# Nested self-attention with ragged lengths: V projected by key tile instead of by head pair

## The chip, the cores and the metric

The kernel runs on one core of a Trainium2 chip. The metric is the device time in microseconds (us) of one execution. Four compute engines work side by side on that core: PE multiplies matrices and writes PSUM, ACT does the exponentials and some copies, DVE does most of the copies out of PSUM and the normalisation, POOL casts inputs. SP and ACT issue the DMAs. PEld is the row of the profile for PE's weight loads, which run beside its matmuls.

## The reference

32 sequences of up to 512 rows and 512 columns; each has a length drawn between 64 and 511, and only its first rows count. Eight heads of 64 columns each.

```python
for b in range(batch):
    seq_len = lengths[b]
    qkv = np.matmul(x[b, :seq_len], w_qkv)
    q, k, v = np.split(qkv, 3, axis=-1)          # then split into 8 heads of 64
    scores = scale * np.matmul(q, k.transpose(0, 2, 1))
    attn = np.exp(scores - np.max(scores, axis=-1, keepdims=True))
    attn = attn / (np.sum(attn, axis=-1, keepdims=True) + 1e-08)
    output[b, :seq_len] = np.matmul(attn, v).transpose(1, 0, 2).reshape(seq_len, dim)
```

Rows past a sequence's length stay zero.

## The kernel before

**Sequences and classes.** The kernel sorts the sequences by length on the chip and takes them in pairs, longest first. Each pair belongs to a class N, the longer length rounded up to a multiple of 32; T is the number of 128-row key tiles in N. For this draw the 16 pairs are: two with T = 4 (N = 512 and 448), six with T = 3 (384, three times 352, 320, 288), six with T = 2 (256, twice 224, 192, twice 160) and two with T = 1 (128, 96). Each class has its own code, a body, which loops while pairs of its class come.

**Halves.** A body does two halves, h = 0 and h = 1, one for each sequence of the pair. In half h the kernel does the attention of sequence h and, between its steps, the projections of the next sequence (g = 1 - h) into the other set of buffers. So what is projected in one half is used in the next.

**Steps.** Within a half the order of PE's work is written out by hand as a string of tokens, `ORDER` for T = 4, 3 and 2 and `DENSE` for T = 3 where three score blocks fit into two PSUM banks (N = 320 and 288):

- `S`: scores of one unit of the current pair of heads into one of two PSUM slots (`psc`, slots s0 and s1), and their exponential by ACT into `ep`. The units come in the order of pairs 1, 2, 3 of this sequence and then pair 0 of the next. `D` does all three key tiles of a pair at once and needs both slots.
- `Q`, `K`: projection of Q or K of one head pair by `qk` (weights are the stationary operand, x the streamed one) into one of two banks of `pa` (a0, a1), and a copy into `qkT`. `B` does Q and K of a pair together. An upper-case letter has the copy done by DVE, a lower-case one by ACT.
- `V`: projection of V by `vproj`, and DVE's copy into `v_aug` with a mask.
- `A`: attention times V of one head pair by `attnv` into `pav`, and DVE's normalisation: a reciprocal and products into `onat`. With T = 3 and 2 the pairs 0 and 1, and 2 and 3, share one normalisation, which follows the odd one. `+` interleaves the matmuls of `A` with those of the step before. With `R` and `X` tokens the normalisation is put at a later place.
- `O`, `P`: ACT waits for the normalisation and issues the store of one half of the columns. With T = 3 and 4 SP issues the second store.

**What orders the engines.** Each projection token takes the other bank of `pa` than the one before it (`st["bank"] ^= 1`), in `group`: PE waits until the bank's last copy is done (`acquire`), does the matmuls, and DVE or ACT waits for them. So each projection waits for the copy of the projection two tokens earlier. Each engine takes its own work strictly in the order of the tokens: ACT's exponentials, copies and the waits of `O` and `P` stand in one queue, as do DVE's copies and normalisations. `pav` has no semaphore of its own; that it is free again follows from the copies that DVE does behind the normalisation.

**V before the change.** `vproj(pr, bank, h, i, T)` does one pair of heads over all T key tiles: T x 4 matmuls that stream 128 columns each, 16 with T = 4, 12 with T = 3 and 8 with T = 2. Four such tokens make up a half. With T = 1 one token does all heads, in 4 matmuls of 512 streamed columns. The matmuls run at line 248 of the profile like all others (a helper); the copy is line 390, with T = 1 line 370; copies of Q and K are line 357 (DVE) and 355 (ACT), exponentials line 290 (in `D` 322), the normalisation lines 447, 469 and 471, the store on ACT line 908.

Of the kernel before, what the change touches and what calls it, by code (L numbers as in the profile page):

```python
# [11 lines left out]
ALU = mybir.AluOpType  # L12

P = 128
NH = 8
HD = 64
# [91 lines left out]
def kernel(  # L108
# [9 lines left out]
    B, MAXS, D = x.shape  # L118
    NT = MAXS // P
    NC = D // P  # L120
# [5 lines left out]
    def sb(name, shape, dt):  # L126
        return nc.alloc_sbuf_tensor(name, shape, dt).ap()
# [5 lines left out]
    w_r = sb("w_r", [P, NC, 3 * D], F16)  # L133
    x_nat = [sb(f"x_nat_{h}", [P, NT, D], FP32) for h in range(2)]
    x16 = [sb(f"x16_{h}", [P, NT, D], F16) for h in range(2)]
    xT = [sb(f"xT_{h}", [P, NC, MAXS], F16) for h in range(2)]
    qkT = [sb(f"qkT_{h}", [P, 2 * NPAIR, MAXS], F16) for h in range(2)]
    v_aug = [sb(f"v_aug_{h}", [P, NT, NH, HD + 1], F16) for h in range(2)]
# [31 lines left out]
    pa = nc.alloc_psum_tensor("pa", [P, 2, MAXS], FP32).ap()  # L170
# [51 lines left out]
    now = [None]  # L222

    def acquire(pr, b):
        if pr.busy.get(b):
            pr.take("pe", free[b])
            pr.busy[b] = False

    def close(pr, b, eng, mms):
        k = len(mms) - 1  # L230
        carry, pr.signals = pr.signals[:k], pr.signals[k:]
        raises = {j: [sem] for j, sem in enumerate(carry)}
        raises[k] = [full[(b, eng)]]
        pr.add("pe", Matmuls(mms, raises))

    def group(pr, b, eng, mms, evac):
        if b in free:
            acquire(pr, b)
        close(pr, b, eng, mms)
        pr.take(eng, full[(b, eng)])  # L240
        if b in free:
            pr.add(eng, lambda e: evac(e).then_inc(free[b], 1))
            pr.busy[b] = True
        else:
            pr.add(eng, evac)

    def mm(o, lhsT, rhs, start, stop):
        return lambda e: e.matmul(o, lhsT, rhs, start=start, stop=stop)  # L248
# [107 lines left out]
        else:  # L356
            group(pr, b, eng, mms, lambda e: e.tensor_copy(out=dst, in_=src))  # L357

    def vproj(pr, bank, h, i, T):
        b = f"a{bank}"  # L360
        mms = []
        if T == 1:
            for c in range(NC):
                mms.append(
                    mm(pa[:, bank, :], xT[h][:, c, 0:P], w_r[:, c, 2 * D : 3 * D],
                       c == 0, c == NC - 1)
                )
            group(
                pr, b, "dve", mms,
                lambda e: e.tensor_scalar(  # L370
                    out=v_aug[h][:, 0, :, 0:HD],
                    in0=pa[:, bank].rearrange("p (h d) -> p h d", d=HD),
                    scalar1=now[0][:, 0, 0:1], scalar2=None, op0=ALU.mult,
                ),
            )
            return
        for t in range(T):
            for c in range(NC):
                mms.append(
                    mm(  # L380
                        pa[:, bank, t * P : (t + 1) * P],
                        xT[h][:, c, t * P : (t + 1) * P],
                        w_r[:, c, 2 * D + i * P : 2 * D + (i + 1) * P],
                        c == 0,
                        c == NC - 1,
                    )
                )
        group(
            pr, b, "dve", mms,
            lambda e: e.tensor_tensor(  # L390
                out=v_aug[h][:, 0:T, 2 * i : 2 * i + 2, 0:HD],
                in0=pa[:, bank, 0 : T * P].rearrange("p (t a d) -> p t a d", a=2, d=HD),
                in1=now[0][:, 0, 0:T].unsqueeze(2).unsqueeze(3).broadcast_to([P, T, 2, HD]),
                op=ALU.mult,
            ),
        )
# [92 lines left out]
    def spread_last(pr):  # L489
# [8 lines left out]
    CANON = {b: True for b in banks}  # L498

    ORDER = {  # L500
# [3 lines left out]
    }  # L504
    DENSE = "D Q0 K0 A0 V0 D Q1 A1 k1 V1 D Q2 K2 A2 V2 D Q3 A3 k3 V3 O"

    ahead = {}

    def read_class(pr, h):
        if h == 0:  # L510
            for g in ("pe", "act", "dve"):
                pr.add(g, lambda e: next_class(e))
# [13 lines left out]
    def half(pr, h, T, N, st):  # L526

        g = 1 - h
        pr.signals += [s_vf[g]] if T == 1 else [s_xtf[h], s_vf[g]]

        def start_proj():
            if not st["x"]:
                st["x"] = True
                pr.take("pe", s_xt[g], 64)
                pr.signals.append(s_x16f[g])

        if T == 1:
            start_proj()
            qk(pr, st["bank"], g, [(i, 0) for i in range(NPAIR)], N, P)
            qk(pr, st["bank"] ^ 1, g, [(i, 1) for i in range(NPAIR)], N, P, "act")  # L540
            read_class(pr, h)
            pr.take("pe", s_on[h])
            attnv(pr, h, 0, 1)
            vproj(pr, st["bank"], g, 0, 1)
            fetch_far(pr, h, N)
            acquire(pr, f"a{st['bank'] ^ 1}")
            pr.signals.append(s_xtf[g])
            scores(pr, h, g, 0, 0, 1, N)
            act_store(pr, h, 0, T)
            st["bank"] ^= 1  # L550
            return
        per = T if T >= 3 else 1
        units = [(i, k) for i in (1, 2, 3, 0) for k in range(per)]
        first, norm, dones = True, {}, 0
        dense = T == 3 and 3 * N <= 2 * MAXS
        toks = (DENSE if dense else ORDER[T]).split()
        for tok in toks:
            k = tok.lstrip("+")[0]
            over, tok = tok != tok.lstrip("+"), tok.lstrip("+")
            i = int(tok[1]) if len(tok) > 1 else 0  # L560
            if k == "S":
                i, kt = units.pop(0)
                scores(pr, st["slot"], g if i == 0 else h, i, kt, T, N)
                st["slot"] ^= 1
            elif k == "D":
                i = units[0][0]
                del units[:T]
                scores_dense(pr, g if i == 0 else h, i, N)
            elif k == "A":
                if first:  # L570
                    first = False
                    pr.take("pe", s_on[h])
                norm[i] = attnv(pr, h, i, T, f"X{i}" in toks)
                if over:
                    spread_last(pr)
            elif k in "RX":
                norm[i][k]()
            elif k in "OP":
                act_store(pr, h, "OP".index(k), T)
            else:  # L580
                start_proj()
                eng = "act" if k.islower() else "dve"
                if k == "V":
                    vproj(pr, st["bank"], g, i, T)
                elif k in "Bb":
                    qk(pr, st["bank"], g, [(i, 0), (i, 1)], N, 256, eng)
                else:
                    qk(pr, st["bank"], g, [(i, "QK".index(k.upper()))], N, MAXS, eng)
                st["bank"] ^= 1

                dones += k != "V"
                if k != "V" and dones == 2:
                    read_class(pr, h)
                elif k != "V" and dones == 3:
                    fetch_far(pr, h, N)
        assert not units
# [63 lines left out]
    def make_prologue():  # L660
        pr = Prog({})
# [104 lines left out]
        bank = 0  # L766
# [34 lines left out]
            pr.add("pe", tr)  # L801
            pr.add(g, back)

        for tok in "Q2 K2 S0 S1 Q3 K3 V0 S2 S3 V1 X2 V2 X3 V3".split():
            f, i = tok[0], int(tok[1])
            if f == "S":
                scores(pr, i % 2, 0, 0, i, 4, MAXS)
                continue
            if f == "X":
                second_batch(i, ("act", "dve")[i % 2])  # L810
                continue
            if f == "V":
                if i == 0:
                    pr.add("pe", lambda e: e.wait_ge(s_wr["v"], 1))
                vproj(pr, bank, 0, i, 4)
            else:
                if i == 2:
                    pr.add("pe", lambda e, n=2 + "QK".index(f): e.wait_ge(s_wr["qk"], n))
                qk(pr, bank, 0, [(i, "QK".index(f))], MAXS, MAXS)
            if tok == "Q2":  # L820
                pr.add("act", cast_v)
            elif tok == "Q3":
                pr.add("pe", lambda e: begin_loops(e))
                cast_second(2)
            elif tok == "K3":
                cast_second(3)
            bank ^= 1
        pr.add("dve", mask_table)
# [47 lines left out]
    def begin_loops(e):  # L876
        e.wait_ge(s_cls, 1)
        r, k = e.alloc_register("pair"), e.alloc_register("cls")
        e.reg_mov(r, 0)
        e.reg_load(k, cls[0:1, 0:1])  # L880
        regs[e.engine] = (r, k)
# [365 lines left out]
```

## Time and profile before

| what | value |
|---|---|
| time, three runs | 364.5, 361.07 and 363.27 us, median 363.27 |
| the profiled execution: span from its first to its last instruction | 359.8 us |
| granted TensorE clock, mean | 0.995 |
| PE busy between 24 and 101 us (T = 4) | 75.70 of 77.00 us |
| PE busy between 101 and 206 us (T = 3, `ORDER`) | 103.28 of 105.00 us |
| PE busy between 206 and 253 us (T = 3, `DENSE`) | 46.22 of 47.00 us |
| PE busy between 253 and 339 us (T = 2) | 82.69 of 86.00 us |
| PE busy between 339 and 353 us (T = 1) | 13.14 of 14.00 us |
| DVE and ACT busy over the span | 232.2 and 228.3 us |

The page of the profile gives a busy time for each engine and for each group of instructions. In a line of a group, the shapes stand before the count, and behind it are the group's busy time in us and the mean duration of one instruction in ns; behind the second bar is the idle time before them and what ended it. A matmul's duration runs from its start to the end of its passage through the array, so durations of consecutive matmuls overlap: what one costs PE is the distance between two starts. In the timeline each line is a run of like instructions: its start, its length to the last one's end, and their number.

### The profile page before, as it was taken

What the parts mean: (1) busy time and instruction counts of PE and PEld (TensorE: products, weight loads), DVE (VectorE), ACT (ScalarE), POOL (GpSimd) and SP (SyncE); (2) the same over time, 40 slices, a digit from 0 to 9 for tenths busy, and PEclk for the clock granted to TensorE, in tenths of its full rate; (3) what the DMA queues carried; (4) which work ended last, traced back from release to release, by engine and by line L of the source; (5) the groups of instructions that cost most, each with busy time, mean ns of one, the idle gap of its engine ahead of it and who ended that gap; (6) DMA issues with size and microseconds to landing.
All of it is one profiled execution on the core that took longest, in us unless ns stands there. A gap on an engine that the chain in (4) does not pass through costs nothing. (4 is left out here: it accounts for less than half of the span.)

```text
span 359.8 us, 12852 instructions
## 1 busy us (share of the span) xinstructions
PE 341.4 (95%) x4896; PEld 246.9 (69%) x4897; DVE 232.2 (65%) x534; ACT 228.3 (63%) x299; POOL 60.8 (17%) x90
## 2 busy tenths in 40 slices
PE   6999999899989999999999999999999999999892
PEld 2566556566656667666666677788879898888761
DVE  3666666566657677676676766576756666676562
ACT  4668778677757667666676667666666565555441
POOL 2614010202010111011011011101112112212120
PEclk9999999999999999999999999999999999999997
DMA  6968998769668766989759749878896856887664
GB/s 196 379 175 272 220 298 229 195 203 171 207 166 237 192 221 202 238 254 293 215 156 318 226 120 305 263 163 192 210 237 180 162 181 161 208 164 215 169 167 111
DMA packets 85127, 76.18 MB, mean 212 GB/s; under 512 B 41552, under 2 KB 64080, under 8 KB 85072
## 3 DMA queue, kind: packets, MB, share of 16 engines
q1 hardware_dynamic: 69952, 60.78, 66.0%
q10 hardware_dynamic: 15120, 14.68, 12.6%
q8 instruction: 33, 0.54, 0.6%
q14 instruction: 22, 0.18, 0.2%
HBM read 29.37 MB, written 36.70 MB: 184 GB/s over the span
## 5 line engine op out<-in xcount | busy, mean ns | idle before, releaser
L290 ACT ACTIVATE ep<-psc 128x704 f16<-128x704 f32 (+4 forms) x217 | 173.9, 852 | 73.8 <-PE psc L248 54.7
L248 PE MATMUL pa<-xT,w_r 128*128 128x352 f16 (+11 forms) x1056 | 164.5, 284 | 1.6 <-DVE qkT L709 0.5
L357 DVE CAST qkT<-pa 128x352 f16<-128x352 f32 (+5 forms) x152 | 85.3, 562 | 58.5 <-PE pa L248 56.6
L248 PEld LDWEIGHTS pa<-xT,w_r 128*128 128x128 f16 x1056 | 82.5, 98 | 45.1 <-issue 19.3
L248 PE MATMUL pa<-w_r,xT 128*128 128x128 f16 (+1 forms) x1296 | 94.9, 221 | 2.1 <-DVE v_aug L390 1.7
L248 PEld LDWEIGHTS pa<-w_r,xT 128*128 128x128 f16 x1296 | 77.2, 98 | 18.1 <-issue 6.3
L248 PE MATMUL pav<-v_aug,ep 128*128 128x65 f16 x1792 | 79.8, 194 | 3.5 <-issue 2.9
L248 PEld LDWEIGHTS pav<-v_aug,ep 128*128 128x128 f16 x1792 | 72.1, 98 | 15.9 <-issue 4.5
L390 DVE TENSOR_TENSOR v_aug<-pa,masks 128x384 f16<-128x384 f32 (+2 forms) x116 | 60.8, 524 | 34.1 <-PE pa L248 29.8
L248 PE MATMUL psc<-qkT 64*128 64x352 f16 (+12 forms) x688 | 66.2, 292 | 1.2 <-PEq L48 1.0
L471 DVE SCALAR_TENSOR_TENSOR onat<-pav,masks,rcp 128x256 f32<-128x256 f32 (+2 forms) x128 | 51.8, 444 | 6.0 <-DVEq L48 1.9
L1119 POOL CAST v_aug<-masks 128x24 f16 (+4 forms) x33 | 9.1, 275 | 267.6 <-POOLq L900 267.6
L1114 POOL CAST x<-x_nat 128x1536 f16<-128x1536 f32 (+3 forms) x33 | 42.1, 1274 | 11.1 <-POOLq L900 10.5
L322 ACT ACTIVATE ep<-psc 128x960 f16<-128x960 f32 (+1 forms) x32 | 28.0, 928 | 16.0 <-PE psc L248 13.5
L248 PEld LDWEIGHTS psc<-qkT 64*128 64x128 f16 x688 | 23.0, 94 | 19.0 <-issue 9.4
L355 ACT CAST qkT<-pa 128x320 f16<-128x320 f32 (+4 forms) x36 | 17.4, 482 | 27.4 <-ACTq L48 17.3
L447 DVE RECIPROCAL rcp<-pav 128x8 f32<-128x8 f32 (+1 forms) x68 | 14.5, 214 | 13.5 <-PE pav L248 10.0
L469 DVE TENSOR_TENSOR onat<-pav,rcp 128x512 f32<-128x512 f32 (+2 forms) x32 | 17.8, 558 | 1.1
L658 PE MATMUL psc<-zt 128*128 128x512 f16 x22 | 6.7, 456 | 1.7 <-DVE zt L1179 1.7
L1125 POOL MEMSET ep<- 128x1024 f32 x6 | 5.4, 955 | 7.4 <-DVE x L719 7.4
L728 ACT CAST w_r<-w_f 128x512 f16<-128x512 f32 (+1 forms) x6 | 4.4, 758 | 3.3 <-DMA w_f<-in_w_qkv_dram 3.3
L658 PEld LDWEIGHTS psc<-zt 128*128 128x128 f16 x22 | 2.3, 113 | 4.3 <-issue 1.7
(58 smaller groups left out, 31.7 us busy)
## 6 DMA issues: line engine op xcount, KB each, us to landing
out_dram<-zt SPq DMA_DIRECT2D x16, 768.0 KB, 6.2
x_nat<-in_x_dram SPq DMA_DIRECT2D x12, 768.0 KB, 5.1
x_nat<-in_x_dram SPq DMA_DIRECT2D x7, 1024.0 KB, 6.7
out_dram<-onat ACTq DMA_DIRECT2D x28, 256.0 KB, 3.7
x_nat<-in_x_dram SPq DMA_DIRECT2D x12, 512.0 KB, 4.2
out_dram<-onat ACTq DMA_DIRECT2D x12, 384.0 KB, 3.3
out_dram<-onat SPq DMA_DIRECT2D x12, 384.0 KB, 3.6
x_nat<-in_x_dram SPq DMA_DIRECT2D x12, 256.0 KB, 3.7
```

The lines of the kernel that those rows point to most:

```text
L248: return lambda e: e.matmul(o, lhsT, rhs, start=start, stop=stop)
L290: lambda e: e.activation(out=dst, in_=src, func=AF.Exp, scale=scale),
L322: lambda e, par=par, b=b: e.activation(out=ep[:, i, par, 0:3, 0:N], in_=psc_f[:, par, 0 : 3 * N].rearrange("p (t n) -> p t n", n=N), func= ...
L355: group(pr, b, eng, mms, lambda e: e.copy(out=dst, in_=src))
L357: group(pr, b, eng, mms, lambda e: e.tensor_copy(out=dst, in_=src))
L390: lambda e: e.tensor_tensor(out=v_aug[h][:, 0:T, 2 * i : 2 * i + 2, 0:HD], in0=pa[:, bank, 0 : T * P].rearrange("p (t a d) -> p t a d", a= ...
L447: pr.add("dve", lambda e: e.reciprocal(out=rv, in_=den).then_inc(s_r, 1))
L469: ins = e.tensor_tensor(op=ALU.mult, **ops)
L471: ins = e.scalar_tensor_tensor(scalar=now[0][:, 1, t : t + 1], op0=ALU.mult, op1=ALU.mult, **ops)
L658: e.matmul(psc[:, 1, 0, :], zt16[:, 0:P], zt16[:, 0:MAXS], start=True, stop=True)
L1114: e.tensor_copy(out=x16[h][:, 0:T, :], in_=x_nat[h][:, 0:T, :]).then_inc(s_xc[h], 1)
L1119: e.tensor_copy(out=v_aug[h][:, 0:T, :, HD], in_=src[:, 0, 0:T].unsqueeze(2).broadcast_to([P, T, NH]),).then_inc(s_on[h], 1)
```

## The change

`vproj` takes a key tile t instead of a head pair i. One token streams all 512 columns of V's weights past one key tile of x, in four matmuls (one for each of the four 128-row chunks of the model dimension), and its copy writes all eight heads of that tile. So a half has T tokens for V instead of four: four with T = 4, three with T = 3, two with T = 2. The separate branch for T = 1 goes. All V tokens of a half must now be done before the first `A` of the next half, where before that held for `V0` alone. The token strings are rearranged, since their number changes and with it the bank that each projection gets; the prologue, which projects the first sequence, has K3 at its end instead of ahead of V0.

```diff
-    def vproj(pr, bank, h, i, T):
+    def vproj(pr, bank, h, t):
         b = f"a{bank}"
-        mms = []
-        if T == 1:
...
-        for t in range(T):
-            for c in range(NC):
-                mms.append(
-                    mm(
-                        pa[:, bank, t * P : (t + 1) * P],
-                        xT[h][:, c, t * P : (t + 1) * P],
-                        w_r[:, c, 2 * D + i * P : 2 * D + (i + 1) * P],
+        mms = [
+            mm(
+                pa[:, bank, :],
+                xT[h][:, c, t * P : (t + 1) * P],
+                w_r[:, c, 2 * D : 3 * D],
+                c == 0,
+                c == NC - 1,
             )
+            for c in range(NC)
+        ]
         group(
             pr, b, "dve", mms,
             lambda e: e.tensor_tensor(
-                out=v_aug[h][:, 0:T, 2 * i : 2 * i + 2, 0:HD],
-                in0=pa[:, bank, 0 : T * P].rearrange("p (t a d) -> p t a d", a=2, d=HD),
-                in1=now[0][:, 0, 0:T].unsqueeze(2).unsqueeze(3).broadcast_to([P, T, 2, HD]),
+                out=v_aug[h][:, t, :, 0:HD],
+                in0=pa[:, bank].rearrange("p (h d) -> p h d", d=HD),
+                in1=now[0][:, 0, t : t + 1].unsqueeze(2).broadcast_to([P, NH, HD]),
                 op=ALU.mult,
             ),
         )
...
     ORDER = {
-        4: "S S Q0 +A0 S S K0 V0 S S Q1 +A1 S S K1 V1 S S Q2 +A2 S S K2 V2 S S Q3 +A3 S S K3 V3 O",
-        3: "S S Q0 A0 K0 S S V0 Q1 A1 S S K1 V1 S S Q2 A2 K2 S S V2 Q3 A3 S S K3 V3 O",
-        2: "S S V0 B0 A0 b1 A1 V1 S S B2 V2 A2 O A3 R3 X3 V3 b3 P",
+        4: "S S Q0 +A0 S S K0 V0 S S Q1 +A1 S S K1 V1 S S Q2 +A2 S S K2 V2 S S Q3 +A3 S S V3 K3 O",
+        3: "S S Q0 A0 K0 S S V0 Q1 S S A1 K1 Q2 S S V1 K2 S S A2 Q3 A3 S S V2 K3 O",
+        2: "S S b0 V0 A0 A1 B1 S S b2 V1 A2 O A3 B3 P",
     }
-    DENSE = "D Q0 K0 A0 V0 D Q1 A1 k1 V1 D Q2 K2 A2 V2 D Q3 A3 k3 V3 O"
+    DENSE = "D Q0 K0 A0 Q1 D A1 k1 V0 Q2 D K2 A2 V1 D Q3 A3 V2 k3 O"
...
-        for tok in "Q2 K2 S0 S1 Q3 K3 V0 S2 S3 V1 X2 V2 X3 V3".split():
+        for tok in "Q2 K2 S0 S1 Q3 V0 S2 S3 V1 X2 V2 X3 V3 K3".split():
```

More of the change, by code (lines that the diff above doesn't have):

```diff
@@ L357, in qk @@
             group(pr, b, eng, mms, lambda e: e.tensor_copy(out=dst, in_=src))
-    def vproj(pr, bank, h, i, T):
+    def vproj(pr, bank, h, t):
         b = f"a{bank}"
-        mms = []
-        if T == 1:
-            for c in range(NC):
-                mms.append(
[L365 to L374, printed above, removed]
-            )
-            return
-        for t in range(T):
-            for c in range(NC):
-                mms.append(
-                    mm(
-                        pa[:, bank, t * P : (t + 1) * P],
-                        xT[h][:, c, t * P : (t + 1) * P],
-                        w_r[:, c, 2 * D + i * P : 2 * D + (i + 1) * P],
[L384 to L387, printed above, removed]
+        mms = [
[5 more added lines that the diff above has]
+                c == NC - 1,
+            )
+            for c in range(NC)
+        ]
         group(
@@ L543, in half @@
             attnv(pr, h, 0, 1)
-            vproj(pr, st["bank"], g, 0, 1)
+            vproj(pr, st["bank"], g, 0)
             fetch_far(pr, h, N)
@@ L583, in half @@
                 if k == "V":
-                    vproj(pr, st["bank"], g, i, T)
+                    vproj(pr, st["bank"], g, i)
                 elif k in "Bb":
@@ L814, in make_prologue @@
                     pr.add("pe", lambda e: e.wait_ge(s_wr["v"], 1))
-                vproj(pr, bank, 0, i, 4)
+                vproj(pr, bank, 0, i)
             else:
@@ L824, in make_prologue @@
                 cast_second(2)
-            elif tok == "K3":
+            elif tok == "V0":
                 cast_second(3)
```

## The prediction

> **What bounds the kernel now.** I read the page first, then the groups by shape, the busy times by stage, and the timeline of single halves.
>
> ```profile
> PE 341.4 (95%) x4896; PEld 246.9 (69%) x4897; DVE 232.2 (65%) x534; ACT 228.3 (63%) x299; POOL 60.8 (17%) x90
> ```
> ```profile
> L248 PE MATMUL pa<-w_r,xT 128*128 128x128 f16 x1280 | 90.8, 219 | 2.1 <-DVE v_aug L390 1.7 <-PEq L48 0.2
> ...
> L390 DVE TENSOR_TENSOR v_aug<-pa,masks 128x512 f16<-128x512 f32 x20 | 13.9, 694 | 3.9 <-PE pa L248 2.8 <-DVEq L48 0.5
> ...
> L248 PE MATMUL pa<-w_r,xT 128*128 128x512 f16 x16 | 4.1, 379 | 0.0
> ...
> L370 DVE TENSOR_SCALAR v_aug<-pa,masks 128x512 f16<-128x512 f32 x4 | 3.0, 746 | 0.0
> ```
>
> PE is busy nearly all the time and DVE and ACT for two thirds, so PE's stream sets the end, and a wait of PE costs what it lasts. V is the first row: 1280 narrow matmuls. What one costs is the distance of two starts, to be had from runs in the timeline:
>
> ```profile
> 160.69 0.83 PE L248 MATMUL pa<-w_r,xT 128*128 128x128 f16 x12
> ...
> 341.52 1.02 PE L248 MATMUL pa<-w_r,xT 128*128 128x512 f16 x4
> ```
>
> Twelve narrow ones take 0.83 us with the last one's 0.219: (0.83 - 0.219) / 11 = 56 ns each. Four wide ones: (1.02 - 0.379) / 3 = 214, and 215.5 by their starts. Four narrow ones cost 224, one wide one 215.5. There is little to gain on PE; the orders decide.
>
> **V's stream.** 1280 x 56 = 71.7 us become 320 x 215.5 = 69.0: -2.7. By stage: T = 4 with the prologue -0.6, `ORDER` T = 3 (8 halves, 12 x 56 x 4 against 12 x 215.5) -0.8, `DENSE` (4 halves) -0.4, T = 2 (12 halves) -0.8, T = 1 none. The weight loads also fall to a quarter; they ran beside the matmuls already.
>
> V's copy now has 512 elements in all classes: 0.69 us by the T = 4 row (same operation; 0.746 by the T = 1 row is the upper end). With T = 3 there are three of 0.69 for four of 0.56, with T = 2 two for four of 0.42, so DVE gains; it is no bound. Score blocks stay at 8, 6, 4 and 2 in a half, so PE's changes between score and full matmuls stay. No load, store, transpose or POOL step is passed by another on SP's or POOL's queue; what moves on ACT's is below.
>
> **T = 2: a copy on ACT comes between two projections of one bank.** New order: S S b0 V0 A0 A1 B1, S S b2 V1 A2 O A3 B3 P. b0 and B1 share a bank, and b0's copy stands on ACT behind the exponentials of its block. Those stand behind P, the store that waits for A3's normalisation. The trace has that hold:
>
> ```profile
> 317.33 0.72 PE L248 MATMUL pa<-xT,w_r 128*128 128x160 f16 x8
> 317.67 0.48 DVE L471 SCALAR_TENSOR_TENSOR onat<-pav,masks,rcp 128x256 f32<-128x256 f32 x1
> 317.98 0.45 PE L248 MATMUL psc<-qkT 64*128 64x160 f16 x8
> 318.06 0.42 DVE L390 TENSOR_TENSOR v_aug<-pa,masks 128x256 f16<-128x256 f32 x1
> 318.09 0.43 ACT L355 CAST qkT<-pa 128x320 f16<-128x320 f32 x1 [1.60 <-PE pa L248]
> 318.38 0.39 ACTq L908 DMA_DIRECT2D out_dram<-onat  x1
> 318.82 1.30 ACT L290 ACTIVATE ep<-psc 128x640 f16<-128x640 f32 x2 [0.30 <-issue]
> ```
>
> The normalisation ends at 318.15, the exponentials of the scores at 317.98 begin at 318.82: 0.67 after it (0.97 where the body loops, 311.53 to 312.51). Today nobody needs a copy by ACT soon after. The second copy of a half also moves ahead of O's store, whose issue (0.38) is over long before P's wait ends.
>
> The walk for N = 160, from the start of the second block: S 0.38, b2 0.56, V1 0.86, A2 and A3 0.49, B3 0.65, so the next half starts at 2.94. V1 ends at 1.80; its copy starts 0.20 later (the lag in the rows) and takes 0.69, to 2.69, and A3's normalisation must queue behind it: reciprocal at 2.75, end after 1.06 (317.09 to 318.15) at 3.81, or 1.24 in the other half. That is 0.87 or 1.04 into the next half; the exponentials start at 1.54 or 2.01, take 1.30, and b0's copy (0.43, with 0.05 before it and 0.06 to PE, as from 284.02 to 284.08) frees the bank at 3.38 or 3.85. B1 wants it at 0.38 + 0.56 + 0.86 + 0.49 = 2.29. PE stands 1.09 or 1.56 us (A1 waits for its own exponential too, at most until 2.8, inside that). The rows of N = 192, 224 and 256 give the same within 0.02, since longer exponentials go with longer projections. Six halves of 1.1, five of 1.57 and the first (behind `DENSE`, no P) of 0.3: +14.7. Behind B1 on PE's queue stand the block's scores, so ACT idles too.
>
> Against it stand today's waits here, narrow V for a bank that V's copy frees late:
>
> ```profile
> PEld pa L248 <- DVE v_aug L390: 5.1, 16, 0.7
> ...
> PE pa L248 <- DVE v_aug L390: 1.7, 6, 0.4
> ```
>
> The weight load's row counts some time in which matmuls still run, PE's row leaves out the passage through the array; the distances of starts lie between: 4.0. They go. T = 2: +14.7 - 4.0 - 0.8 = +9.9.
>
> **T = 3, `ORDER`: V1 waits for K1's copy.** Now the second normalisation sits ahead of three projections: A1 K1 Q2, S S V1, and V1 takes K1's bank.
>
> ```profile
> 159.78 0.23 DVE L447 RECIPROCAL rcp<-pav 128x12 f32<-128x12 f32 x1
> ...
> 160.05 0.69 DVE L469 TENSOR_TENSOR onat<-pav,rcp 128x512 f32<-128x512 f32 x1
> ...
> 160.66 0.47 DVE L471 SCALAR_TENSOR_TENSOR onat<-pav,masks,rcp 128x256 f32<-128x256 f32 x1
> ...
> 161.05 0.51 DVE L357 CAST qkT<-pa 128x352 f16<-128x352 f32 x1
> ```
>
> Normalising takes 1.35 us in half 0, 1.65 in half 1 (146.84 to 148.49). From K1's start: reciprocal at 0.20, K1's copy done at 0.20 + 1.35 - 0.08 + 0.51 = 1.98, bank free at 2.04 (2.34). V1 wants it after K1 0.60, Q2 0.60, the change to scores 0.10 and S S 0.40: 1.70. Wait 0.35 and 0.65; with N = 384 (longer projections) 0.26 and 0.55. Sum of eight halves +3.8. Gone is the shortest distance of two score blocks, 1.77 us, just what two exponentials need; it becomes 1.97, and seven late score blocks (0.46 to 0.57 us instead of 0.40, one V 0.22 longer) lose 0.9. T = 3: +3.8 - 0.9 - 0.8 = +2.1.
>
> **`DENSE`: two such waits.** D A1 k1 V0 Q2: k1's copy on ACT stands behind D's exponentials and ends 2.79 us after D's start (209.41 to 212.20):
>
> ```profile
> 209.41 0.58 PE L248 MATMUL psc<-qkT 64*128 64x320 f16 x8
> ...
> 210.02 1.83 ACT L322 ACTIVATE ep<-psc 128x960 f16<-128x960 f32 x2 [1.12 <-PE psc L248]
> ...
> 211.77 0.43 ACT L355 CAST qkT<-pa 128x320 f16<-128x320 f32 x1
> ```
>
> Q2 wants the bank at D 0.51 + A1 0.56 + k1 0.54 + V0 0.86 = 2.48: with the lag 0.37 (N = 320), 0.28 (N = 288). And V2, behind A3's normalisation, is copied late for the next half's Q0: A3 ends at 1.62, normalising at 3.17 or 3.47, the copy at 3.78 or 4.08; Q0 wants it at 3.64: 0.20 or 0.50, with N = 288 about 0.1 more. Sum 1.3 + 1.5, less 0.4 for V and 0.2 for a late block: +2.2.
>
> T = 4 keeps its order but for the last two tokens: V3's copy ends 2.3 us after the last A, the next Q0 comes at 2.9; nothing. The prologue's V0 comes 0.95 us earlier, still 0.9 after its weights (cast until 17.45): nothing.
>
> **Sum.** -0.6 + 2.1 + 2.2 + 9.9 = +13.6 on the span of 359.8: 373.4. The execution profiled has no other time than its span; the median of the runs lies 3.5 above it (their spread is 3.4), taken as what lies around it. **377 us**, 3.8% slower.
>
> What the trace does not show: fewer instructions may shift the fetch waits at a class's first pass (PE "issue" up to 1.6, 1.5, and 1.0 at 230): -4 if all go, +3 if two come; I take 0.
>
> **Rivals.**
> - *P does not hold the exponentials* (ACT starts them with the scores, 0.41 in, as at 272.94). Then b0's copy is ready 2.78 after the block's start (N = 224) against 2.62 wanted, T = 2 has 2.7 of waits instead of 14.7, and the sum is +1.6: 365, no change to speak of. It decides from a normalisation that ends before the next scores. For it: V's copies are half as many. Against it: the hold is in both rows above, and V1's copy now stands right ahead of the normalisation. 13%.
> - *Narrow V costs PE more than its starts show.* By busy times 90.8 / 1280 x 4 = 284 ns against 4.1 / 16 = 256: -8.8 instead of -2.7, 371. Against it: busy counts the last one's passage. 7%.
> - *Far more*: waits that feed on each other (B3 for b2, B's copies behind late normalisations), another 0.6 in each T = 2 half: 384. 9%.
> - *Wide streams hide weight loads.* If a load stood between narrow matmuls, V would lose up to 98 ns x 960 = 94 us, and the kernel would be faster, 286 at the least. The starts 56 ns apart leave no room for it: 1%. The Trainium skill, TensorE: Matmul & The Clock Gate, Back-to-back issue gap, gives about 81 ns for a sustained narrow matmul and 131 for a wide one; by it V would gain 1280 x 81 - 320 x 131 = 62 us (an estimate from that page). The trace has 56 and 215.5, and it decides.
>
> **Chances.** The forecast 70%. Its own range is 371 to 383. The range 366 to 383 leaves out the last two rivals and most of the first, 2 in 10. A change of 1% (3.6 us) is about what a measurement tells from none: slower 85%, within 1% 11% (the first rival and little fetch), faster 4%.
>
> **What would show it.** In T = 2 PE idles before the B projections, released by ACT's copy into `qkT`, about 14 us in all; in `ORDER` T = 3 before V1, released by DVE's copy into `qkT`, 0.3 to 0.7 each; in `DENSE` before Q2 (ACT) and Q0 (DVE, `v_aug`). The stage of T = 2 grows from 86 to about 96 us, T = 3 from 152 to 156. Wide V 215 ns apart. Wrong if the exponentials of T = 2 start within 0.5 us of their scores, or if B1 follows A1 at once.

## The result, and the profile after

| | before | after |
|---|---|---|
| median of four runs each | 363.2 us (361.07 to 364.5) | 374.69 us (374.36 to 377.36) |
| ratio, with its 95% interval | | 1.0343 (1.0293 to 1.0393) |
| the profiled execution: its time, its span | | 374.81 us, 373.0 us |

The change makes the kernel 3.4% slower. The span came out at 373.0 us where the sum gave 373.4, and the time at 374.7 where I said 377. To see where the 13.2 us of span went, I cut both traces at the first score matmul of each class. The last column is the prediction's sum for the same stage.

| stage, us | before | after | difference | predicted |
|---|---|---|---|---|
| prologue and T = 4 | 101.03 | 100.14 | -0.9 | -0.6 |
| T = 3, `ORDER` (384, 352) | 105.43 | 106.38 | +0.95 | +2.1 |
| T = 3, `DENSE` (320, 288) | 46.81 | 48.60 | +1.8 | +2.2 |
| T = 2 | 85.47 | 94.88 | +9.4 | +9.9 |
| T = 1, to the end | 21.03 | 23.02 | +2.0 | 0 |

First the engines' row on the page of the kernel after (busy us, share of the span, instructions).

```profile
PE 343.9 (92%) x3936; PEld 203.4 (55%) x3937; DVE 224.6 (60%) x498; ACT 225.9 (61%) x299; POOL 60.8 (16%) x90
```

PE has 960 matmuls fewer, but its busy share fell from 95 to 92%: PE now waits. The 960 fewer weight loads take 43 us off PEld's row, but the kernel is no faster for it. Wide V and its copy are these groups of the kernel after (busy us, mean ns of one, then the idle time before them and what ended it):

```profile
L248 PE MATMUL pa<-w_r,xT 128*128 128x512 f16 x336 | 86.6, 380 | 4.4 <-DVE qkT L357 4.4
...
L373 DVE TENSOR_TENSOR v_aug<-pa,masks 128x512 f16<-128x512 f32 x84 | 58.1, 692 | 59.1 <-PE pa L248 48.1 <-DVEq L48 10.2
```

Before, V's two rows had 90.8 and 4.1 us of busy time with 2.1 us of idle ahead of them, 1.7 of it ended by V's own copy. Now 4.4 us of idle time stand ahead of V, ended by DVE's copy of Q or K: the wait has a new owner. Starts within wide V lie 215 to 216 ns apart, as taken, and the copy takes 0.692 us (0.69).

**T = 2.** The waits of the kernel after between 255 and 350 us (total us, times, longest):

```profile
ACT ep L290 <- ACTq L48: 32.8, 16, 2.8
...
PEld pa L248 <- ACT qkT L355: 8.6, 12, 0.9
...
PE pa L248 <- ACT qkT L355: 7.2, 12, 0.8
...
PEld pa L248 <- DVE qkT L357: 2.4, 6, 0.6
```

Twelve halves, twelve waits of PE for a copy by ACT. The first row is mostly the store: ACT idles in its own queue (ACTq) ahead of the exponentials, for 32.8 us; with the second store taken off ACT (run 2) 9.5 us are left. One half of N = 224 in the timeline of the kernel after, from the normalisation that the store waits for:

```profile
288.55 0.88 DVE L454 SCALAR_TENSOR_TENSOR onat<-pav,masks,rcp 128x256 f32<-128x256 f32 x2
288.71 0.56 PE L248 MATMUL psc<-qkT 64*128 64x224 f16 x8
...
289.20 0.94 PE L248 MATMUL pa<-xT,w_r 128*128 128x224 f16 x8
...
290.45 1.73 ACT L290 ACTIVATE ep<-psc 128x896 f16<-128x896 f32 x2 [2.74 <-ACTq L48]
290.89 0.96 PE L248 MATMUL pav<-v_aug,ep 128*128 128x65 f16 x16
...
292.06 0.54 ACT L355 CAST qkT<-pa 128x448 f16<-128x448 f32 x1
...
292.66 0.75 PE L248 MATMUL pa<-xT,w_r 128*128 128x224 f16 x6 [0.81 <-ACT qkT L355]
```

The scores start at 288.71, their exponentials at 290.45, 1.02 us after the normalisation's end at 289.43. Behind them stands b0's copy, until 292.60, and B1, which wants b0's bank, starts at 292.66. This is the chain that the prediction walked for N = 160, at its predicted place.

**T = 3.** V1 waits for K1's copy, which DVE does behind the second normalisation (timeline of the kernel after, N = 352):

```profile
132.66 1.36 PE L248 MATMUL pa<-xT,w_r 128*128 128x352 f16 x8
...
133.74 0.47 DVE L454 SCALAR_TENSOR_TENSOR onat<-pav,masks,rcp 128x256 f32<-128x256 f32 x1
133.96 0.47 PE L248 MATMUL psc<-qkT 64*128 64x352 f16 x4
134.13 0.94 DVE L357 CAST qkT<-pa 128x352 f16<-128x352 f32 x2
...
134.71 1.04 PE L248 MATMUL pa<-w_r,xT 128*128 128x512 f16 x4 [0.28 <-DVE qkT L357]
```

The eight matmuls at 132.66 are K1 and Q2; K1's copy begins at 134.13, as the normalisation ends on DVE. By distances of starts these waits are 0.25 and 0.54 us with N = 384, 0.35 and 0.64 with N = 352, 3.75 in all; the prediction had 0.26, 0.55, 0.35, 0.65 and 3.8.

**`DENSE`** has the two waits foreseen (Q2 for k1's copy 1.0 us in all; Q0 for V2's copy 1.7, of which 0.6 is b0's, the first projection of T = 2, and falls into the next stage; predicted 1.3 and 1.5) and a third that was not, of about 1.0 us in all. Timeline of the kernel after, N = 320:

```profile
218.54 0.58 PE L248 MATMUL psc<-qkT 64*128 64x320 f16 x8
...
219.84 0.46 ACTq L891 DMA_DIRECT2D out_dram<-onat  x1
...
220.34 1.83 ACT L322 ACTIVATE ep<-psc 128x960 f16<-128x960 f32 x2 [1.27 <-issue]
...
222.31 0.59 PE L248 MATMUL psc<-qkT 64*128 64x320 f16 x8 [0.71 <-ACT ep L322]
```

k3 was ahead of O before, too, but now V2 is ahead of k3. So ACT comes to its store late, issues it when D's scores are already done, and starts their exponentials 1.8 us after the scores began (0.62 at the same place before the change, where the store was issued with the scores); the next D waits for both slots.

### The profile page after: what moved, and what is told of

The parts are those of the page before. It is cut to its first block, busy times and chain, and to the rows that moved or that the text cites. A ratio compares the mean times of both kernels' runs of the same rounds, so it can differ in the third digit from the quotient of the medians.

```text
span 373.0 us, 10946 instructions
## 1 busy us (share of the span) xinstructions
PE 343.9 (92%) x3936; PEld 203.4 (55%) x3937; DVE 224.6 (60%) x498; ACT 225.9 (61%) x299; POOL 60.8 (16%) x90
## 5 line engine op out<-in xcount | busy, mean ns | idle before, releaser
L357 DVE CAST qkT<-pa 128x352 f16<-128x352 f32 (+5 forms) x152 | 84.4, 560 | 57.7 <-PE pa L248 56.0
L248 PEld LDWEIGHTS pa<-xT,w_r 128*128 128x128 f16 x1056 | 85.6, 99 | 59.2 <-issue 14.6
L373 DVE TENSOR_TENSOR v_aug<-pa,masks 128x512 f16<-128x512 f32 x84 | 58.1, 692 | 59.1 <-PE pa L248 48.1
L248 PE MATMUL pa<-w_r,xT 128*128 128x512 f16 x336 | 86.6, 380 | 4.4 <-DVE qkT L357 4.4
L248 PEld LDWEIGHTS pav<-v_aug,ep 128*128 128x128 f16 x1792 | 70.4, 98 | 22.3 <-issue 6.4
L248 PE MATMUL pav<-v_aug,ep 128*128 128x65 f16 x1792 | 78.8, 194 | 1.4 <-issue 1.2
L248 PEld LDWEIGHTS pa<-w_r,xT 128*128 128x128 f16 x336 | 28.8, 98 | 38.4 <-DVE qkT L357 8.5
```

Of the source, the lines that this page charges most:

```text
L373: lambda e: e.tensor_tensor(out=v_aug[h][:, t, :, 0:HD], in0=pa[:, bank].rearrange("p (h d) -> p h d", d=HD), in1=now[0][:, 0, t : t + 1]. ...
```

## The experiments

My theory of the loss was the prediction's: T = 2 loses most of it, because ACT's store holds the exponentials and b0's copy behind them. Rivals: wide V itself costs PE time; the loss sits in the order of DVE's queue, whoever copies b0; the shifted instruction fetches do it. All orders below are token strings, and each diff is against the kernel after.

**1. T = 2 alone undone (t2_old).** T = 2 gets its old order and V by head pair back (`vpair` is the old `vproj`).

```diff
-        2: "S S b0 V0 A0 A1 B1 S S b2 V1 A2 O A3 B3 P",
+        2: "S S V0 B0 A0 b1 A1 V1 S S B2 V2 A2 O A3 R3 X3 V3 b3 P",
...
-                    vproj(pr, st["bank"], g, i)
+                    if T == 2:
+                        vpair(pr, st["bank"], g, i, T)
+                    else:
+                        vproj(pr, st["bank"], g, i)
```

> The changed kernel with T = 2 alone put back: V by head pair and the old order there, all else as changed. If the waits of the new T = 2 order are the loss of that stage, it goes from 94.9 to about 85.5 us, and PE no longer stands 1.7 us before the T = 1 stage, so the half clock there goes as well: time about 363 (374.7 - 9.4 - 2). If the drop of the clock in T = 1 has nothing to do with T = 2, about 365. If the loss sits in T = 3 and not here, over 370.

Measured: 365.49 us, ratio to the kernel before 1.0096 (1.0061 to 1.0131). T = 2 takes 85.34 us, as before the change (85.47). So T = 2 holds 9.5 us of the loss. The pause ahead of T = 1 fell to 1.17 us and the clock stayed full there, as expected, but T = 1 stayed 1.6 us longer than before. In its place the profile has a longer pause of PE's sequencer in N = 96, which the kernel before does not have:

```profile
354.97 1.52 PE L248 MATMUL pa<-xT,w_r 128*128 128x96 f16 x32 [2.21 <-PEq L48]
```

So the time came near the 365 of the second case by another way than that case had.

**2. The store's hold taken away (t2_sp).** Without `P`, SP issues the second store as with T = 3 and 4.

```diff
-        2: "S S b0 V0 A0 A1 B1 S S b2 V1 A2 O A3 B3 P",
+        2: "S S b0 V0 A0 A1 B1 S S b2 V1 A2 O A3 B3",
```

> The changed kernel without P: in T = 2 the second store is issued by SP, as with T = 3 and 4, so ACT's exponentials no longer queue behind a wait for the normalisation. My theory (the hold by P delays the exponentials, these delay b0's copy, B1 waits for it): the exponentials start 0.4 after their scores, B1 waits 0 to 0.6 instead of 0.5 to 1.3, T = 2 takes about 84 us, time about 363. Rival (DVE is what is late: V's copy and the normalisation ahead of the copies that PE waits for): ACT's queue does not matter, T = 2 stays above 92, time above 371.

Measured: 370.38 us, 1.0234 (1.0198 to 1.027); T = 2 takes 88.26 us instead of 94.88. Its timeline, a half of N = 224:

```profile
287.49 0.56 PE L248 MATMUL psc<-qkT 64*128 64x224 f16 x8
287.50 0.88 DVE L454 SCALAR_TENSOR_TENSOR onat<-pav,masks,rcp 128x256 f32<-128x256 f32 x2
287.90 1.73 ACT L290 ACTIVATE ep<-psc 128x896 f16<-128x896 f32 x2 [1.42 <-PE psc L248]
```

The exponentials start 0.41 us after their scores, in the middle of the normalisation, and it is PE that they waited for. The hold costs 6.6 us. Still, T = 2 is 2.8 us slower than before, and above the 84 us that were expected.

**3. b0 and b2 copied by DVE instead (t2_dve).** The hold stays, but nobody on PE waits for a copy behind it.

```diff
-        2: "S S b0 V0 A0 A1 B1 S S b2 V1 A2 O A3 B3 P",
+        2: "S S B0 V0 A0 A1 B1 S S B2 V1 A2 O A3 B3 P",
```

> The changed kernel with b0 and b2 copied by DVE instead of ACT, P where it is. My theory: B1 no longer waits for a copy on ACT, but the exponentials are still held by P, so A1 waits for its own exponential by 0.3 to 0.7 in each half: about 5.5 us of waits in T = 2 instead of 14, T = 2 about 86, time 365 to 367. Rival (DVE is what is late): two more copies of 0.5 on DVE make it worse, T = 2 above 95, time above 374.

Measured: 368.87 us, the median of the three runs behind the ratio (a fourth took 374.15), 1.0205 (1.0145 to 1.0264); T = 2 takes 88.33 us, more than the 86 expected and the same as with the store moved. Either end of the chain cut, the same 6.6 us come back; so it is one chain, as walked.

**4. Both together (t2_dve_sp).** The two edits above in one string.

```diff
-        2: "S S b0 V0 A0 A1 B1 S S b2 V1 A2 O A3 B3 P",
+        2: "S S B0 V0 A0 A1 B1 S S B2 V1 A2 O A3 B3",
```

> The changed kernel with both single edits of T = 2 at once, its order kept: b0 and b2 copied by DVE and the second store on SP. Each alone left the stage at 88.3 us (85.5 before the change). If what is left is the place of the normalisation behind V's copy, which makes B3's copy late for the next V0, the order must change and both edits together give 87 to 88; V0's wait of 0.2 to 0.6 at N = 192 and 160 stays. If the two queues are the whole loss, 83 to 84.

Measured: 369.93 us, 1.0222 (1.0169 to 1.0274); T = 2 takes 88.19 us. Together they give no more than each alone, so what is left of the loss (2.7 us) has another cause. The timeline of this kernel, at the end of a half, shows it:

```profile
299.36 0.69 DVE L373 TENSOR_TENSOR v_aug<-pa,masks 128x512 f16<-128x512 f32 x1 [0.63 <-DVEq L48]
...
299.97 0.20 DVE L430 RECIPROCAL rcp<-pav 128x8 f32<-128x8 f32 x1
...
300.31 0.88 DVE L454 SCALAR_TENSOR_TENSOR onat<-pav,masks,rcp 128x256 f32<-128x256 f32 x2
...
301.11 1.08 DVE L357 CAST qkT<-pa 128x448 f16<-128x448 f32 x2
...
301.78 0.39 PE L248 MATMUL pa<-w_r,xT 128*128 128x512 f16 x1 [0.20 <-DVE qkT L357]
```

On DVE, V1's copy stands ahead of A3's normalisation, and B3's copy behind it. The next V0, at 301.78, wants B3's bank. V1 waits in the same way for B1's copy, which stands behind A1's normalisation, and that behind V0's copy. By distances of starts PE loses up to 0.6 us at such a place, 1.7 us in all before V0 and 3.1 before V1 (part of the latter ends, by the profile, in PE's own sequencer).

**5. T = 2 in a new order (t2_new).** V goes behind the `A` tokens, so that the normalisation comes first on DVE; the store is on SP.

```diff
-        2: "S S b0 V0 A0 A1 B1 S S b2 V1 A2 O A3 B3 P",
+        2: "S S B0 A0 A1 V0 B1 S S B2 A2 O A3 V1 B3",
```

> The changed kernel with T = 2 as S S B0 A0 A1 V0 B1 S S B2 A2 O A3 V1 B3: all copies on DVE, the second store on SP, V behind the attention, so that the normalisation does not queue behind V's copy. After the two single edits, each of which left 2.8 us more than before the change, I hold that both queues cost: ACT's hold 6.6 us, DVE's late copy of B3 (V0 waits 0.2 to 0.6) the rest. Then T = 2 takes 81 to 83 us (94.9), time 12 below the changed kernel. If DVE is simply too full with all copies, T = 2 stays at 87 or more.

Measured: 363.59 us, 1.0026 (0.9997 to 1.0055); T = 2 takes 85.14 us, above the 81 to 83 that were expected. Two pauses of PE in its own sequencer (0.9 and 1.1 us) are in it, which the same order does not show in run 8, where it takes 82.74. The order gives 3.1 to 5.5 us over run 4 with the same work.

**6. V narrow in the orders of after (narrow).** Each wide V matmul is cut into four of 128 columns, and nothing else changes.

```diff
-                pa[:, bank, :],
+                pa[:, bank, j * P : (j + 1) * P],
...
-                w_r[:, c, 2 * D : 3 * D],
+                w_r[:, c, 2 * D + j * P : 2 * D + (j + 1) * P],
...
+            for j in range(D // P)
             for c in range(NC)
```

> The changed kernel with each wide matmul of V cut into four of 128 columns: same tokens, banks, copies and orders, only the streams as narrow as before. By the distances of starts (56 ns against 215.5 for four times the columns) it costs 2.7 us, of which the 0.8 of T = 2 can hide in the waits there: time 376.5 to 377.5. If wide streams hide weight loads that narrow ones show, it costs 10 us and more. If the instruction count brings the fetch waits at a class's first pass back, another 2.6.

Measured: 377.38 us, 1.0418 (1.0373 to 1.0464). From the first score of T = 4 to the end of T = 2 it takes 2.45 us more than the kernel after (335.55 against 333.10), near the 2.7 that the starts of V's matmuls give. So the weight loads that went are worth no more than this.

**7. T = 3 in new orders (t3_new, dense_new).** In both, more of PE's work stands between a copy that must come late and the projection that takes its bank. `t3_new`:

```diff
-        3: "S S Q0 A0 K0 S S V0 Q1 S S A1 K1 Q2 S S V1 K2 S S A2 Q3 A3 S S V2 K3 O",
+        3: "S S Q0 K0 A0 S S Q1 K1 A1 S S Q2 V0 S S V1 A2 S S K2 Q3 A3 S S K3 V2 O",
```

> The changed kernel with another order for T = 3: S S Q0 K0 A0 S S Q1 K1 A1 S S Q2 V0 S S V1 A2 S S K2 Q3 A3 S S K3 V2 O. Behind a normalisation comes a score block and two projections before one wants a bank whose copy stands behind it. If V1's wait for K1's copy is all that the old order lost, the 3.75 us of it go: the stage of N = 384 and 352 from 106.4 to 102.6, time 3.7 below the changed kernel. If the loss is in the fewer, wider copies themselves, the stage stays.

`dense_new`:

```diff
-    DENSE = "D Q0 K0 A0 Q1 D A1 k1 V0 Q2 D K2 A2 V1 D Q3 A3 V2 k3 O"
+    DENSE = "D Q0 K0 A0 Q1 D A1 k1 V0 D Q2 K2 A2 V1 D Q3 A3 k3 V2 O"
```

> The changed kernel with another DENSE: Q2 behind the third D, k3 ahead of V2 (D Q0 K0 A0 Q1 D A1 k1 V0 D Q2 K2 A2 V1 D Q3 A3 k3 V2 O). My theory: Q2's wait for k1's copy on ACT (1.0 us in sum), Q0's for V2's copy (1.7) and the late exponentials behind O's store (about 1) go, the stage of N = 320 and 288 goes from 48.6 to 45 to 46, time 3 below the changed kernel. If D's own slots bind (blocks shorter than two exponentials), it stays above 47.5.

Measured: `t3_new` 372.12 us, 1.0255 (1.0193 to 1.0317), `ORDER` T = 3 in 102.73 us for 106.38. `dense_new` 372.02 us, 1.0247 (1.0192 to 1.0302), `DENSE` in 45.78 us for 48.60. The 3.65 us match the predicted V1 waits, the 2.8 us most of the `DENSE` waits. With `t3_new` the time fell by 2.6 us where 3.7 were expected: its profiled execution has a pause of 2.06 us and a stretch of half clock in T = 4, which takes 2.5 us longer.

**8. The three new orders together (best).** The strings of runs 5 and 7, with K3 in place of k3 in `DENSE`.

```diff
-        3: "S S Q0 A0 K0 S S V0 Q1 S S A1 K1 Q2 S S V1 K2 S S A2 Q3 A3 S S V2 K3 O",
-        2: "S S b0 V0 A0 A1 B1 S S b2 V1 A2 O A3 B3 P",
+        3: "S S Q0 K0 A0 S S Q1 K1 A1 S S Q2 V0 S S V1 A2 S S K2 Q3 A3 S S K3 V2 O",
+        2: "S S B0 A0 A1 V0 B1 S S B2 A2 O A3 V1 B3",
...
-    DENSE = "D Q0 K0 A0 Q1 D A1 k1 V0 Q2 D K2 A2 V1 D Q3 A3 V2 k3 O"
+    DENSE = "D Q0 K0 A0 Q1 D A1 k1 V0 D Q2 K2 A2 V1 D Q3 A3 K3 V2 O"
```

> V by key tile with all three new orders (T = 3, T = 2 as in the single runs; DENSE with K3 copied by DVE instead of k3, which costs Q0 up to 0.3 in half 1). If the waits are the whole loss and add up, it is 3.7 + 2.5 + 12 below the changed kernel: about 356, 2% faster than the kernel before. If the wide V is a loss in itself, it does not get below the kernel before.

Measured: 357.19 us over six runs (355.85 to 358.88), ratio to the kernel before 0.9853 (0.981 to 0.9896): 1.5% faster than the kernel before. Its page:

```profile
PE 337.3 (95%) x3936; PEld 203.2 (57%) x3937; DVE 241.0 (68%) x526; ACT 214.9 (61%) x271; POOL 60.6 (17%) x90
```

PE's busy share is back at 95%. The end of a half of N = 224 in its timeline:

```profile
268.15 0.47 DVE L454 SCALAR_TENSOR_TENSOR onat<-pav,masks,rcp 128x256 f32<-128x256 f32 x1
268.19 0.93 PE L248 MATMUL pa<-xT,w_r 128*128 128x224 f16 x8
268.55 0.69 DVE L373 TENSOR_TENSOR v_aug<-pa,masks 128x512 f16<-128x512 f32 x1
269.05 0.56 PE L248 MATMUL psc<-qkT 64*128 64x224 f16 x8
269.16 0.62 DVE L357 CAST qkT<-pa 128x448 f16<-128x448 f32 x1
269.46 1.73 ACT L290 ACTIVATE ep<-psc 128x896 f16<-128x896 f32 x2 [1.76 <-PE psc L248]
```

Normalisation, V1's copy, B3's copy, in this order, and the last one is done 0.73 us after the next scores start; the exponentials follow their scores by 0.41. By stage against before: T = 2 -2.7, `ORDER` T = 3 -2.7 (1.5 of it a fetch wait that is gone, below), T = 4 -0.6, `DENSE` and T = 1 within 0.2.

**9. The same with narrow V (best_narrow).** The edit of run 6 on the kernel of run 8.

> The version with all new orders, each wide matmul of V cut into four of 128 columns. With few waits left for it to hide in, the width is worth the distance of starts: 320 x (4 x 56 - 215.5 ns) = 2.7 us, time about 360. If the wide stream only helped by moving waits, the two are the same.

Measured: 360.5 us over twelve runs, 0.9951 (0.9923 to 0.998). The two ratios differ by 1.0%, some 3.5 us, and their intervals do not overlap. In the profiled executions the stages from T = 4 to T = 2 grow by 2.0 us, the prologue by 1.0, and T = 1 by 2.2 with a pause of PE's sequencer. So of the 5.3 us that run 8 gains, the width carries between 2.0 and 3.5. The rest is the fetch wait that went in T = 3 and the new order of T = 2, where narrow V takes 84.2 us for 85.5 before. Whether V by head pair, with its four tokens, could gain as much from a new order was not tried.

## Why the prediction was right, and where it was not

- **PE bounds the kernel, and a wait of PE costs what it lasts.** Shown: runs 2 to 5 and 7 took waits away and the stages shrank by them.
- **V's stream, -2.7.** Right: 215 to 216 ns by the starts, 2.45 us by run 6. The Trainium skill, TensorE: Matmul & The Clock Gate, Back-to-back issue gap, has other spacings for sustained matmuls, by which V would gain about 62 us (an estimate from that page). The runs disagree with it: 4 x 56 against 215.5 ns, and 2.45 us for the width.
- **T = 2: +14.7 of waits, -4.0, -0.8.** The mechanism is shown, the sum is right (+9.4 for +9.9), the terms were each somewhat large. By distances of starts against those of unhindered matmuls, the waits behind the `A` runs grew by 10.7 us (B1 0.5 to 1.3 a half, about 10 in all; the rest B3), and 2.0 us stand before V0, which waits for B3's copy. That is 12.7 for 14.7. The chain splits at the smaller classes: what V0 already lost, B1 no longer loses. V's old waits gave back 3.1 instead of 4.0, and the last pause before T = 1 grew by 0.6. The 0.6 of b0 that the prediction has in `DENSE` came here, and 0.7 of smaller old waits went. Run 4 adds what the prediction gave only to a rival, B's copies behind late normalisations: without ACT's hold PE loses 4.8 us at these places, and T = 2 stays 2.7 us above before, with V's old waits and 0.8 us of V's stream already given back.
- **T = 3, `ORDER`: +3.8 of V1 waits.** Right to a few hundredths of a microsecond. The stage came out at +0.95 for +2.1, because a fetch wait of 1.5 us at the class's first pass went; without that it is +2.4. The gain of 0.9 from late score blocks was too large: by what is left it was about 0.5.
- **`DENSE`: +2.2.** +1.8 measured, but with a fetch wait of 0.8 us gone, so +2.6. The term missing is the store O behind k3 (1.0 us): I costed Q2's and Q0's waits and never asked what k3's later copy does to the store, and the store to D's exponentials.
- **T = 1: nothing.** Failed: +2.0 us. In the profiled execution the 32 narrow matmuls of the first Q and K after T = 2 take 3.36 us instead of 1.95, at half the granted clock; see the last section. 1.6 us of it are in N = 128. Two of the other three executions have a mean clock of 0.995 and 0.996, against 0.989 here, which leaves little room for such a stretch, and took 374.4 and 374.6 us all the same; what they lost in its place is not known.
- **What lies around the span.** I took 3.5 us from the median of three runs; the profiled execution after has 374.81 - 373.0 = 1.8. Most of the 2.3 us between 377 and 374.7 is this.
- **Fetch waits, taken as 0.** -2.3 us by the two that went, inside the range given (-4 to +3). With T = 1's +2.0 it almost cancels: that the span came within 0.4 us of the sum is luck.

The rival that P does not hold the exponentials is refuted by the timeline above and by run 2. Even where ACT does not hold them, as in run 2, T = 2 loses 2.8 us; that rival's sum for the stage, 2.7 - 4.0 - 0.8, was a gain of 2.1.

## What to carry to other kernels

When a change alters how many tokens rotate through two banks, walk each new pair of neighbours on a bank: whose copy frees it, what stands ahead of that copy in its engine's queue, and when. A store that waits on the queue of a compute engine is harmless until somebody soon needs what stands behind it; cutting either end of such a chain gives the same gain, and doing both gives no more. A restructuring that loses may still pay: its own gain was some 2.5 us of stream, and it showed only when the orders were written for the new waits.

## What the runs showed of the hardware that I had not expected

**Half the clock after a short pause.** The entry into T = 1 in the timeline of the kernel after:

```profile
347.73 0.72 PE L248 MATMUL pa<-xT,w_r 128*128 128x160 f16 x8
350.02 0.40 PE L248 MATMUL psc<-qkT 64*128 64x128 f16 x8 [1.58 <-PEq L48]
350.75 3.36 PE L248 MATMUL pa<-xT,w_r 128*128 128x128 f16 x32 [0.33 <-PEq L48]
```

and the same place before the change:

```profile
337.02 0.72 PE L248 MATMUL pa<-xT,w_r 128*128 128x160 f16 x8
338.75 0.40 PE L248 MATMUL psc<-qkT 64*128 64x128 f16 x8 [1.01 <-PEq L48]
339.48 1.95 PE L248 MATMUL pa<-xT,w_r 128*128 128x128 f16 x32 [0.33 <-PEq L48]
```

PE stood 1.58 us in its sequencer, and a microsecond later its clock is 0.50 for 3.4 us. In each of the twelve traces the changes of the clock lie whole multiples of 3.41 us apart, so I cut PE's time into such steps. Two of them in the kernel after (length; busy us and count of PE, PEld, DVE, ACT and POOL; granted clock; DMA share; GB/s):

```profile
347.61:351.02 3.41, 1.51 (x31) 1.19 (x28) 2.08 (x5) 0.47 (x1) 0.00 (x0) 1.00 0.44 157
351.02:354.43 3.41, 3.41 (x40) 3.41 (x37) 0.69 (x1) 0.76 (x2) 0.83 (x2) 0.50 0.47 94
```

and two in t2_old, around its pause of 2.21 us:

```profile
350.45:353.86 3.41, 2.32 (x41) 1.50 (x37) 2.16 (x4) 1.29 (x2) 0.65 (x2) 1.00 0.98 129
353.86:357.27 3.41, 2.30 (x44) 1.94 (x44) 0.77 (x2) 0.48 (x1) 0.83 (x2) 1.00 0.78 169
```

In the kernel after the pause lies within one step, in which PE idles for 1.90 us, and the next step has half the clock. The longer pause of t2_old is cut by the border at 353.86 into two steps with 1.09 and 1.12 us idle, and the clock stays full. So the length of a pause alone does not decide. At the entry into T = 1 five traces (the kernel before, t2_old, t2_new, best and best_narrow) have a pause of 1.01 to 1.17 us and full clock behind it. Seven have one of 1.57 to 1.68; in five of them the clock halves at once and N = 128 takes 8.7 us, in the other two (t2_sp, t2_dve_sp) it takes 7.2, and the clock halves after a second pause, of 2.22 and 1.95 us, in N = 96. It does so, too, after pauses of 2.06 us in T = 4 (t3_new) and 1.98 us in N = 96 (best_narrow). Counted by steps, between 25 us and the last matmul, each of the nine with 1.89 us or more of idle is followed by half the clock, and none with 1.68 us or less is. The Trainium skill, TensorE: Matmul & The Clock Gate, What's actually happening, has the clock fall after an idle window of about 3.4 us. The slow stretch here is as long (3.4 us), but a window of idle alone was not needed: 1.9 us of idle within a step was enough. No run set the pause alone, so that idle time within a step is the cause is argued from these places, not tested.

**Fetch waits move with the code.** At the first pass of a class PE stood 1.47 us in N = 384 and, by distances of starts, 0.8 in N = 288 before the change, not after it; t2_new got two of 0.9 and 1.1 us in N = 224 and N = 192, t2_sp and t2_old one of 2.2 in N = 96. They follow no part of the change that I could name, and came to some 2 us between kernels that differ in one string. That they are instruction fetches is my reading; the profile names nothing but PE's own sequencer, or no releaser at all. The Trainium skill, Runtime: NRT & Kernel Launch, Instruction fetch mechanics, says that a taken branch to code outside the window fetched costs a stall; places at the classes' first passes agree with it, and no run here isolates it.
